# Lower weight halves of every second gate and up chunk, made by a ScalarE negation and an adding DMA

## The chip, the core and the metric

The kernel runs as one program on one core of a Trainium2 chip. The metric is the device time of one execution in microseconds (us). Before the change the median of 3 runs is 1681.12 us.

## What is computed

One layer of a decoder trunk on 256 tokens of width 2048, all in float32. Cut to what the change touches, it is

```python
h = h + _mixer(_rmsnorm(h, norm_mix[l]), ...)          # linear attention and convolution, merged
h = h + _swiglu(_rmsnorm(h, norm_ffn[l]), w_gate[l], w_up[l], w_down[l])

def _swiglu(h, w_gate, w_up, w_down):
    return (jax.nn.silu(h @ w_gate) * (h @ w_up)) @ w_down
```

The hidden width of the second part (the FFN) is 5632. `w_gate` and `w_up` are 2048 x 5632 each, 92 MB together.

## The kernel before

**Products in two parts.** TensorE takes its operands in a rounded float32 format (float32r in the code). To keep float32 accuracy every weight w is split into `hi` (w rounded to float32r) and `lo = w - hi`, every activation likewise, and three products are summed: hi.hi, hi.lo and lo.hi. In the form used by the gate and up weights (form "M"), a weight tile of 128 x 128 is held stationary; `hi` is multiplied with both halves of the activations at once (512 columns, L223), `lo` with the upper half alone (256 columns, L224).

**The weight stream.** The weights lie packed in HBM in groups of 2048 columns on 128 partitions, 1024 KB each. SyncE's queue (SP) loads one group by one DMA into a tile `raw` (L165); there are three such tiles (`RAW = 3`). A group holds two chunks of 1024 columns, and a chunk is the unit of all that follows. For each chunk ScalarE (ACT) makes `hi` by a casting copy (L175), VectorE (DVE) makes `lo` by a subtraction `raw - hi` (L177), and TensorE (PE) then runs 16 products on it, 2 rows of weight tiles by 4 tiles of output, each with its pair L223 and L224. `hi` and `lo` have five tiles each (`LOOK + 1`), so chunk i takes the tile of chunk i - 5 and can be split as soon as PE has finished that one, four chunks ahead of its use.

**The FFN.** Eleven blocks of 512 gate columns alternate with eleven blocks of up columns. A block runs over 2048 rows, that is 8 chunks or 4 groups, so gate and up together are 176 chunks in 88 groups. Behind the last chunk of a block stand four evacuations: ACT copies half of a bank (`ms`, L252), DVE adds the other half (`mt`, L256), multiplies by the norm, and ACT applies silu (`gt`) for gate, or ACT and DVE split the product into `hs` for up. The down projection that follows takes its weights from the same stream.

**What sets the order.** `run_blocks` writes, for each chunk of products, first the load and split of the chunk four ahead (`load_next`), then the products. A tile framework places the instructions on the engines and adds semaphore waits; each engine works its own list in order. GpSimd (POOL) does next to nothing: constants and four masks.

Of the kernel before, what the change touches and what calls it, by code (L numbers as in the profile page):

```python
# [8 lines left out]
F32 = mybir.dt.float32  # L9
F32R = mybir.dt.float32r  # L10
AF = mybir.ActivationFunctionType
ALU = mybir.AluOpType

P = 128
T = 256
D = 2048
KT = D // P
# [4 lines left out]
NB = 512  # L22
Q0, K0, V0, R0, A0, U0, G0, GA0, GB0 = 0, 1024, 2048, 4096, 6144, 6160, 8208, 10256, 12304
P_MIX, P_CB, P_LG, P_LB, P_PB, P_GN, P_NF, P_BA = [i * 16 for i in range(8)]
LOOK = 4     # chunks of weights split ahead of the products
RAW = 3      # groups of weights in flight
NA = 60      # slots of 2 KB for activations
NS = 8       # single-tile chunks at the start
WARM = 10    # products that bring the tensor engine to its clock
# background work let in per chunk, in the unit of the steps' costs  # L30
BUD, BG, BO = 1.22, 0.95, 1.05


# [1 line left out]
def trunk(ctx: ExitStack, tc, xT, par, convw, ws, wal2, nfin, out):  # L35
# [21 lines left out]

    v, sc, pe = nc.vector, nc.scalar, nc.tensor

# [1 line left out]
    pr = cpool.tile([P, 8 * 16], F32, tag="pr", name="pr")  # L61
    nc.scalar.dma_start(pr, par)
    ones = cpool.tile([P, P], F32, tag="ones", name="ones")
# [20 lines left out]
        return pr[:, off + i:off + i + 1]  # L84

    def split(dst, src):
        """dst [P, 512] F32R = (hi | lo) of src [P, 256]"""
        sc.copy(dst[:, 0:T], src)
        v.tensor_tensor(dst[:, T:2 * T], src, dst[:, 0:T].bitcast(F32), op=ALU.subtract)  # L89

# [1 line left out]
    tick = [0]  # L92
    order = {}
    done = set()

    class Work:
        """steps run in order; a step with a delay waits that many chunks after the one before"""

        def __init__(self):
            self.steps, self.last = deque(), 0  # L100
# [31 lines left out]
            q = gla_w_ if gla_w_.ready() else conv_w_  # L132
            credit[0] -= q.step()

# [1 line left out]
    # Products of float32: both operands split exactly into hi + lo float32r parts, summed as  # L136
    # hi.hi + hi.lo + lo.hi. Form "M": weights stationary, one bank holds W_hi.x_hi beside
    # W_hi.x_lo + W_lo.x_hi; form "S": the three in one region; form "A": x stationary.
    blocks = []

    def add_block(width, nk, form, xs, evac, before=None, budget=BUD):
        blocks.append(dict(width=width, nk=nk, form=form, xs=xs, evac=evac,
                           before=before, budget=budget))

    loads = []
    staged = {}
    nload = [0]
    raws = {}

    def load_next():  # L150
        i = nload[0]
        if i >= len(loads):
            return
        nload[0] += 1
        g, e, n, k, kp, width = loads[i]
        first = i < len(blocks[0]["chunks"])
        if 0 < i and first:
            x_load(k, kp)
        if first or e == 0:
            # a whole group of two chunks at once, but for the first block  # L160
            size = n if first else 2 * n
            raw = (atile([P, NB], s="raw") if kp == 1 else
                   wpool.tile([P, 4 * NB], F32, tag="raw", name=nm("raw"), bufs=RAW))
            with tc.issue_after(order["s"]) if "s" in order else nullcontext():
                d = nc.sync.dma_start(raw[:, 0:size], ws[g, :, e:e + size])  # L165
            raws["t"] = raw
            if i == 0:
                order["s"] = d.ins
        r0 = 0 if first else e
        r = raws["t"][:, r0:r0 + n]  # L170
        if i == 0:
            x_load(k, kp)
        hi, lo = (wpool.tile([P, kp, width], F32R, tag=t, name=nm(t)) for t in ("hi", "lo"))
        fl = lambda t: t.rearrange("p k n -> p (k n)")
        order["a"] = sc.copy(fl(hi), r).ins  # L175
        gs = [x_gain(j) for j in range(k, k + kp)] if first else []
        order["v"] = v.tensor_tensor(fl(lo), r, fl(hi).bitcast(F32), op=ALU.subtract).ins  # L177
        for x in gs:
            XU.append(atile([P, 2 * T], F32R, "xu"))
            with tc.issue_after(order["a"]), tc.issue_after(order["v"]):  # L180
                split(XU[-1], x)
        staged[i] = (hi, lo)

    def run_blocks():
        group = 0
        for b in blocks:
            b["first"] = len(loads)
            kp = 2 * NB // b["width"]
            b["chunks"] = [(k, kp) for k in range(0, b["nk"], kp)]
            if b is blocks[0]:  # L190
                b["chunks"] = [(k, 1) for k in range(NS)] + b["chunks"][NS // 2:]
            for k, kp in b["chunks"]:
                at = k * b["width"]
                loads.append((group + at // (4 * NB), at % (4 * NB), kp * b["width"], k, kp, b["width"]))
            group += b["nk"] * b["width"] // (4 * NB)
        for b in blocks:
# [49 lines left out]
                    pump(b["budget"])  # L246

    def merged_sum(a, bias=None):
        """the two halves of a bank, added"""
        t1 = ttile("ms")  # L250
        if bias is None:
            sc.copy(t1, a[:, 0:T])  # L252
        else:
            sc.activation(t1, a[:, 0:T], AF.Identity, bias=bias)
        t2 = ttile("mt")
        v.tensor_tensor(t2, a[:, T:2 * T], t1, op=ALU.add)  # L256
        return t2

    def rms_bcast(dst, acc_t, mat, eps):
        """dst = 1 / sqrt(column sums of acc_t through mat + eps), on every partition"""  # L260
        m = misc()
        pe.matmul(m[:, 0:T], lhsT=mat, rhs=acc_t, start=True, stop=True)  # L262
        s = ttile("rs")
        sc.activation(s, m[:, 0:T], AF.Sqrt, bias=eps)
        v.reciprocal(dst, s)

# [1 line left out]
    xp = []  # L268
    XU = []
    X = []  # L270
# [53 lines left out]
            X.append(s)  # L324
        return f

# [1 line left out]
    U = {}  # L328
    YC = {}
    US = {}  # L330
# [31 lines left out]
        return f  # L362

    def conv(p):
        """channel tiles 2p and 2p + 1, taps in turns"""
        def first(j):
            def f():
                if j == 0:
                    YC[p] = atile([P, 2, T], s="yc")
                i = 2 * p + j  # L370
                sc.activation(YC[p][:, j, :], u_tile(i), AF.Identity,
                              scale=cw[:, i, CW - 1:CW], bias=pcol(P_CB, i))
            return f

        def tap(d, j):
            def f():
                i = 2 * p + j
                y = YC[p][:, j, :]
                v.scalar_tensor_tensor(y[:, d:T], in0=u_tile(i)[:, 0:T - d],  # L379
                                       scalar=cw[:, i, CW - 1 - d:CW - d], in1=y[:, d:T],  # L380
                                       op0=ALU.mult, op1=ALU.add)
            return f
        conv_w_.add(0.0, first(0))
        conv_w_.add(0.0, first(1))
        for d in range(1, CW):
            for j in range(2):
                conv_w_.add(0.37, tap(d, j))
# [54 lines left out]
            conv_w_.add(1.3, scale(i))  # L442
        conv_w_.mark("conv")

# [1 line left out]
    QK = {}  # L446
    VT = {}
    SR = {}
# [37 lines left out]
        return t.rearrange("p j (c s) -> p (j c) s", s=64)  # L486

    def gla_att(h):
        """the masked, decayed scores of head h, keys on partitions"""
        st = ST[h]  # L490

        def z():
# [51 lines left out]
                sc.activation(dq[:, j], even[:, j], AF.Exp, scale=-1.0 / 16)  # L544
            st.update(dk=dk, dq=dq, qs=[], ks=[])

        # b: log decay from a chunk's start; the pair of chunks 0, 1 and the pair 2, 3 meet at
        # the border inside the pair, queries 2, 3 and keys 0, 1 at the border between the pairs
        def queries(j):
            def f():  # L550
                eb, q = (t[:, j, :].rearrange("p (c s) -> p c s", s=64) for t in (st["eb"], QK["q", h]))
                dq = st["dq"][:, j]
                a = atile([P, 6, 64], s="qs")
                # q0 -> border, q1, q2 -> border, q3, q2, q3 from chunk 2's start
                v.tensor_tensor(a[:, 0:4:2, :], q[:, 0::2, :], dq, op=ALU.mult)
                v.tensor_tensor(a[:, 1:4:2, :], q[:, 1::2, :], eb[:, 1::2, :], op=ALU.mult)
                v.tensor_tensor(a[:, 4, :], q[:, 2, :], eb[:, 2, :], op=ALU.mult)
# [4 lines left out]
        def prods(j):  # L562
            def f():
# [1 line left out]
                             for t in (st["eb"], st["dk"], QK["k", h]))  # L565
                en = st["en"][:, j]
                a = atile([P, 6, 64], s="ks")
                # kd0 ke1 kd0' kd1 kd2 ke3
                v.tensor_tensor(a[:, 0::4, :], k[:, 0::2, :], dk[:, 0::2, :], op=ALU.mult)
                v.tensor_tensor(a[:, 1::4, :], k[:, 1::2, :], en, op=ALU.mult)  # L570
                v.tensor_tensor(a[:, 3, :], k[:, 1, :], dk[:, 1, :], op=ALU.mult)
# [4 lines left out]
        def att():  # L576
            m = misc()
            qs, ks = st.pop("qs"), st.pop("ks")
            # keys 0:128 by queries 0:128, keys 128:256 by queries 128:256, keys 0:128 by queries 128:256
            for c, ko, qo in ((0, 0, 0), (1, 4, 2), (2, 2, 4)):  # L580
                for j in range(2):
                    pe.matmul(m[:, c * P:(c + 1) * P], lhsT=ks[j][:, ko:ko + 2, :],  # L582
# [21 lines left out]
        gla_w_.add(0.0, att, 2)  # L604

    def gla_out(h):
        """head h's output and its norm"""
        st = ST[h]

        def outp(pp):  # L610
# [49 lines left out]
            gla_w_.add(1.0, gate(e), 1)  # L660
        gla_w_.mark(("gla", h))

# [1 line left out]
    SGA, SGB = {}, {}  # L664
    MG = {}
    XR = {}
# [80 lines left out]
    def ffn_gate_evac(blk):  # L747
        def f(n, a):
            gla_w_.drain("rstd2")
            t = merged_sum(a)  # L750
            g = ttile("fg")
            v.tensor_tensor(g, t, rstd, op=ALU.mult)
            GT[n] = tpool.tile([P, T], F32, tag="gt", name=nm("gt"), bufs=5)
            sc.activation(GT[n], g, AF.Silu)
        return f
# [50 lines left out]
                nc.sync.dma_start(out[n * P:(n + 1) * P, m * NB:(m + 1) * NB], o)  # L806
        return f

# [1 line left out]
    xu = lambda: XU  # L810
    xx = lambda: X

# [39 lines left out]
    for blk in range(4):  # L852
        add_block(NB, KT, "M", lambda: MG, out_evac(blk), before=out_before(blk))
    for blk in range(11):
        add_block(NB, KT, "M", lambda: Y2, ffn_gate_evac(blk), budget=0.01)
        add_block(NB, KT, "M", lambda: Y2, ffn_up_evac(blk), budget=0.01)
    for nb in range(4):
        add_block(NB, HT, "A", lambda: HS, down_evac(nb),
                  before=down_before if nb == 0 else None, budget=0.0)
# [60 lines left out]
```

## Time and profile before

| | |
|---|---|
| median of 3 runs | 1681.12 us (1680.71 to 1681.37) |
| span of the profiled execution, first to last instruction | 1678.7 us |
| products of gate and up chunks | from 929.2 to 1430.2 us in the span |
| PE busy | 1666.4 us, 99% |
| DVE busy | 1219.4 us, 73% |
| ACT busy | 883.3 us, 53% |
| POOL busy | 4.5 us, 10 instructions |

The profiled execution's own time is given by its span; 2.4 us of the median lie around it. The page lists busy time by engine, the chain of work that ended last (followed back from the last instruction through what released each step), the costliest groups of instructions with the idle time before them, and the DMA queues. Idle time of an engine counts only where it lies on that chain.

### The profile page before, as it was taken

The numbers are of one execution on the slowest core, as the hardware profiler recorded it, in microseconds if no ns is written. First come the engines' busy times: TensorE is split into PE (matmuls) and PEld (weight loads), VectorE is DVE, ScalarE is ACT, GpSimd is POOL, SyncE is SP. The second block draws the span as 40 slices with busy tenths as digits, with TensorE's granted clock in tenths as the row PEclk, the third lists the DMA queues.
The fourth block names the chain that finished last, engine by engine and source line by source line (L and its number), as shares of the span: only waits on it lengthen the run. The fifth ranks groups of instructions, "written<-read, shape, count | busy, mean of one in ns | idle before, by whom it ended". The sixth has DMA issues, their size and how long they took to land.

```text
span 1678.7 us, 23321 instructions
## 1 busy us (share of the span) xinstructions
PE 1666.4 (99%) x9140; PEld 1437.8 (86%) x9140; DVE 1219.4 (73%) x1945; ACT 883.3 (53%) x1293; POOL 4.5 (0%) x10
## 2 busy tenths in 40 slices
PE   9999999999999999999999999999999999999997
PEld 7888888888888888888888888888888888888886
DVE  7898899888879899886777666666666666554453
ACT  6654444666766655584555654444444444444343
POOL 0000000000000000000000000000000000000000
PEclk9999999999999999999999999999999999999999
DMA  8555555554444445555555545555454555655552
GB/s 301 185 201 189 188 184 190 181 186 177 166 173 174 173 177 195 182 184 195 199 206 214 182 176 194 181 188 189 180 196 176 194 182 186 215 201 191 188 198 100
DMA packets 48413, 316.45 MB, mean 189 GB/s; under 512 B 5392, under 2 KB 6672, under 8 KB 11312
## 3 DMA queue, kind: packets, MB, share of 16 engines
q1 hardware_dynamic: 48160, 314.91, 52.2%
q8 instruction: 71, 1.16, 0.3%
q14 instruction: 38, 0.31, 0.1%
q10 hardware_dynamic: 144, 0.07, 0.0%
HBM read 312.86 MB, written 2.10 MB: 188 GB/s over the span
## 4 chain that ended last, share of the span: by engine, by line
PE 99%; DMA 0%; DVE 0%; ACT 0%; issue 0%; ACTq 0%; SPq 0%; DVEq 0%
PE acc L223 52%; PE acc L224 26%; PE acc L216 7%; PE acc L217 6%; PE acc L218 6%; PE m L582 0%; PE m L497 0%; PE m L619 0%; PE m L620 0%; DMA x<-in_xT_dram 0%; PE m L618 0%; PE m L740 0%; PE m L262 0%; PE acc L228 0%; PE acc L227 0%; PE acc L229 0%
## 5 line engine op out<-in xcount | busy, mean ns | idle before, releaser
L177 DVE TENSOR_TENSOR lo<-raw,hi 128x1024 fp32r<-128x1024 f32 (+1 forms) x590 | 717.1, 1216 | 412.2 <-ACT hi L175 406.1
L175 ACT CAST hi<-raw 128x1024 fp32r<-128x1024 f32 (+1 forms) x590 | 616.4, 1046 | 730.3 <-PE acc L223 523.2
L223 PE MATMUL acc<-y2s,hi 128*128 128x512 f32 x1408 | 498.4, 399 | 0.0
L223 PE MATMUL acc<-xs,hi 128*128 128x512 f32 x1280 | 450.5, 397 | 0.0
L224 PE MATMUL acc<-y2s,lo 128*128 128x256 f32 x1408 | 395.3, 281 | 0.0
L224 PE MATMUL acc<-xs,lo 128*128 128x256 f32 x1280 | 357.0, 279 | 0.0
L223 PEld LDWEIGHTS acc<-y2s,hi 128*128 128x128 f32 x1408 | 264.6, 188 | 65.4
L223 PEld LDWEIGHTS acc<-xs,hi 128*128 128x128 f32 x1280 | 240.3, 188 | 57.5 <-ACT hi L175 0.3
L224 PEld LDWEIGHTS acc<-y2s,lo 128*128 128x128 f32 x1408 | 265.9, 189 | 0.0
L224 PEld LDWEIGHTS acc<-xs,lo 128*128 128x128 f32 x1280 | 241.1, 188 | 0.1
L379 DVE SCALAR_TENSOR_TENSOR yc<-u,cw,yc 128x255 f32<-128x255 f32 (+14 forms) x480 | 199.6, 463 | 0.1
L216 PE MATMUL acc<-hi,hs 128*128 128x512 f32 x352 | 137.0, 389 | 0.0
L218 PE MATMUL acc<-hi,hs 128*128 128x512 f32 x352 | 136.9, 389 | 0.0
L217 PE MATMUL acc<-lo,hs 128*128 128x512 f32 x352 | 136.9, 389 | 0.0
L223 PE MATMUL acc<-xu,hi 128*128 128x512 f32 x256 | 90.3, 398 | 2.4 <-DVE xu L89 2.4
L223 PE MATMUL acc<-ogs,hi 128*128 128x512 f32 x256 | 89.3, 394 | 0.0
L223 PE MATMUL acc<-mgs,hi 128*128 128x512 f32 x256 | 88.8, 394 | 0.0
L223 PE MATMUL acc<-us,hi 128*128 128x512 f32 x256 | 88.8, 394 | 0.0
L256 DVE TENSOR_TENSOR mt<-acc,ms 128x256 f32<-128x256 f32 x200 | 81.6, 417 | 7.7 <-ACT ms L252 7.7
L218 PEld LDWEIGHTS acc<-hi,hs 128*128 128x128 f32 x352 | 66.1, 188 | 13.9
L216 PEld LDWEIGHTS acc<-hi,hs 128*128 128x128 f32 x352 | 66.1, 188 | 13.7
L217 PEld LDWEIGHTS acc<-lo,hs 128*128 128x128 f32 x352 | 66.1, 188 | 13.6
(176 smaller groups left out, 1607.4 us busy)
## 6 DMA issues: line engine op xcount, KB each, us to landing
raw<-in_weights_dram SPq DMA_DIRECT2D x289, 1024.0 KB, 4.8
raw<-in_weights_dram SPq DMA_DIRECT2D x8, 256.0 KB, 4.5
raw<-in_weights_dram SPq DMA_DIRECT2D x4, 512.0 KB, 7.0
xr<-in_xT_dram SPq DMA_DIRECT2D x8, 256.0 KB, 5.2
out_dram<-fin SPq DMA_DIRECT2D x8, 256.0 KB, 3.1
x<-in_xT_dram SPq DMA_DIRECT2D x8, 128.0 KB, 4.7
x<-in_xT_dram SPq DMA_DIRECT2D x4, 256.0 KB, 7.0
nf<-in_norm_final_dram SPq DMA_DIRECT2D x4, 256.0 KB, 6.6
```

Source lines behind the costliest of these rows:

```text
L175: order["a"] = sc.copy(fl(hi), r).ins
L177: order["v"] = v.tensor_tensor(fl(lo), r, fl(hi).bitcast(F32), op=ALU.subtract).ins
L216: pe.matmul(a, lhsT=xh[:, t], rhs=hi[:, kk, :], start=st, stop=False)
L217: pe.matmul(a, lhsT=xh[:, t], rhs=lo[:, kk, :], start=False, stop=False)
L218: last = pe.matmul(a, lhsT=xl[:, t], rhs=hi[:, kk, :], start=False, stop=en)
L223: pe.matmul(a, lhsT=wh, rhs=x, start=st, stop=False)
L224: last = pe.matmul(a[:, T:2 * T], lhsT=wl, rhs=xh, start=False, stop=en)
L256: v.tensor_tensor(t2, a[:, T:2 * T], t1, op=ALU.add)
L379: v.scalar_tensor_tensor(y[:, d:T], in0=u_tile(i)[:, 0:T - d], scalar=cw[:, i, CW - 1 - d:CW - d], in1=y[:, d:T], op0=ALU.mult, op1=ALU.add)
```

## The change

In gate and up blocks (`dma=True`), for the second chunk of each group (`k // kp % 2 == 1`), the subtraction on DVE is gone. In its place ACT writes `lo = -hi` by an activation with scale -1, and POOL's queue then issues a DMA from SBUF to SBUF that adds `raw` to `lo`. The first chunk of each group is split as before. 88 chunks are changed. The adding DMAs are kept in order among themselves. The diff also drops comments, which shifts line numbers (L177 becomes L184); those hunks are left out here.

```diff
-    def add_block(width, nk, form, xs, evac, before=None, budget=BUD):
+    def add_block(width, nk, form, xs, evac, before=None, budget=BUD, dma=False):
         blocks.append(dict(width=width, nk=nk, form=form, xs=xs, evac=evac,
-                           before=before, budget=budget))
+                           before=before, budget=budget, dma=dma))
...
         order["a"] = sc.copy(fl(hi), r).ins
         gs = [x_gain(j) for j in range(k, k + kp)] if first else []
-        order["v"] = v.tensor_tensor(fl(lo), r, fl(hi).bitcast(F32), op=ALU.subtract).ins
+        if by_dma[i]:
+
+            order["a"] = sc.activation(fl(lo), fl(hi).bitcast(F32), AF.Copy, scale=-1.0).ins
+            with tc.issue_after(order["g"]) if "g" in order else nullcontext():
+                order["g"] = nc.gpsimd.dma_start(fl(lo).bitcast(F32), r, accum_op=ALU.add).ins
+        else:
+            order["v"] = v.tensor_tensor(fl(lo), r, fl(hi).bitcast(F32), op=ALU.subtract).ins
...
             for k, kp in b["chunks"]:
                 at = k * b["width"]
+                by_dma.append(b["dma"] and k // kp % 2 == 1)
...
-        add_block(NB, KT, "M", lambda: Y2, ffn_gate_evac(blk), budget=0.01)
-        add_block(NB, KT, "M", lambda: Y2, ffn_up_evac(blk), budget=0.01)
+        add_block(NB, KT, "M", lambda: Y2, ffn_gate_evac(blk), budget=0.01, dma=True)
+        add_block(NB, KT, "M", lambda: Y2, ffn_up_evac(blk), budget=0.01, dma=True)
```

**ACT's list behind the end of an up block.** `hi_1904` and `hi_1910` are the two chunks of one group, `ms` and `hs` belong to the block that ends. Names in brackets are the semaphores that an instruction waits for: those with DMAHW are of SP's loads, those with DMASW of POOL's DMAs. Before:

```order
L175 CAST hi_1904_10228<-raw_1903_10226 128x1024 [waits DMAHW3_49,DVE_49,PE_49]
L88 CAST hs_1887_10178<-hd_1886_10176 128x256 [waits DVE_49]
L252 COPY ms_1888_10185<-acc_1863_10021 128x256
L175 CAST hi_1910_10252<-raw_1903_10226 128x1024 [waits PE_49,Activation_49]
L252 COPY ms_1893_10200<-acc_1864_10026 128x256 [waits Activation_49]
L88 CAST hs_1892_10193<-hd_1891_10191 128x256 [waits DVE_49]
L175 CAST hi_1913_10274<-raw_1912_10272 128x1024 [waits DMAHW4_49,PE_49]
```

With the change:

```order
L176 CAST hi_1904_10246<-raw_1903_10244 128x1024 [waits DMAHW3_49,PE_49]
L260 COPY ms_1893_10218<-acc_1864_10040 128x256 [waits Activation_49]
L88 CAST hs_1892_10211<-hd_1891_10209 128x256 [waits DVE_49]
L176 CAST hi_1910_10270<-raw_1903_10244 128x1024 [waits PE_49]
L260 COPY ms_1898_10233<-acc_1865_10045 128x256 [waits Activation_49]
L88 CAST hs_1897_10226<-hd_1896_10224 128x256 [waits DVE_49]
L180 ACTIVATE lo_1911_10271<-hi_1910_10270 128x1024 [waits DMASW5_49,PE_49,Activation_49]
L176 CAST hi_1913_10293<-raw_1912_10291 128x1024 [waits DMAHW4_49,PE_49]
```

One negation stands behind each second cast, here with one `ms` and one `hs` between the two; elsewhere in a block it follows the cast directly.

**SP's list of loads, at the same place.** Before, a load waits for the loads and for DVE, which is the last reader of the `raw` tile that it fills:

```order
L165 DMA raw_1873_10098<-in_weights_dram 128x2048 [waits DMAHW6_49,DVE_49]
L165 DMA raw_1878_10140<-in_weights_dram 128x2048 [waits DMAHW7_49,DVE_49]
L165 DMA raw_1903_10226<-in_weights_dram 128x2048 [waits DMAHW0_49,DVE_49]
L165 DMA raw_1912_10272<-in_weights_dram 128x2048 [waits DMAHW1_49,DVE_49]
L165 DMA raw_1917_10314<-in_weights_dram 128x2048 [waits DMAHW2_49,DVE_49]
```

With the change:

```order
L166 DMA raw_1873_10114<-in_weights_dram 128x2048 [waits DMASW5_49,DMAHW6_49,DVE_49,Activation_49]
L166 DMA raw_1878_10157<-in_weights_dram 128x2048 [waits DMASW6_49,DMAHW7_49,DVE_49,Activation_49]
L166 DMA raw_1903_10244<-in_weights_dram 128x2048 [waits DMASW7_49,DMAHW0_49,DVE_49,Activation_49]
L166 DMA raw_1912_10291<-in_weights_dram 128x2048 [waits DMASW0_49,DMAHW1_49,DVE_49,Activation_49]
L166 DMA raw_1917_10334<-in_weights_dram 128x2048 [waits DMASW1_49,DMAHW2_49,DVE_49,Activation_49]
```

Each load now waits for an adding DMA too: the one that reads the old contents of its `raw` tile, three groups back.

## Rows read from the trace of the kernel before

**Rows 1.** The page: busy us (share of the span) xinstructions; the chain's first line.

```profile
PE 1666.4 (99%) x9140; PEld 1437.8 (86%) x9140; DVE 1219.4 (73%) x1945; ACT 883.3 (53%) x1293; POOL 4.5 (0%) x10
...
PE 99%; DMA 0%; DVE 0%; ACT 0%; issue 0%; ACTq 0%; SPq 0%; DVEq 0%
```

**Rows 2.** Stretches of the span: window, then columns as its first line names them.

```profile
core 0: us, PE busy (x) PEld busy (x) DVE busy (x) ACT busy (x) POOL busy (x), PEclk, DMA share, GB/s
...
640.00:670.00 30.00, 30.00 (x175) 26.25 (x174) 28.34 (x53) 15.66 (x24) 0.00 (x0) 1.00 0.52 181
...
760.00:790.00 30.00, 30.00 (x175) 26.23 (x174) 19.16 (x27) 14.37 (x19) 0.00 (x0) 1.00 0.54 194
...
935.00:1430.00 495.00, 495.00 (x2818) 429.94 (x2817) 309.24 (x435) 241.29 (x358) 0.00 (x0) 1.00 0.52 185
```

**Rows 3.** Groups of instructions, 935 to 1430 us: busy us, mean ns | idle before, releasers.

```profile
L177 DVE TENSOR_TENSOR lo<-raw,hi 128x1024 fp32r<-128x1024 f32 x174 | 213.2, 1225 | 181.1 <-ACT hi L175 179.0
L175 ACT CAST hi<-raw 128x1024 fp32r<-128x1024 f32 x174 | 182.8, 1050 | 248.0 <-PE acc L223 230.2 <-issue 14.1 <-PE acc L224 2.1
...
L252 ACT COPY ms<-acc 128x256 f32<-128x256 f32 x86 | 31.3, 364 | 2.3 <-PE acc L224 2.3
...
L88 ACT CAST hs<-hd 128x256 fp32r<-128x256 f32 x40 | 16.2, 406 | 1.2 <-PE acc L224 1.2
...
L716 ACT ACTIVATE hq<-h 128x512 f32<-128x512 f32 x1 | 0.6, 629 | 0.0
```

**Rows 4.** ACT's timeline in an FFN block: start us, us, instruction, idle before.

```profile
1198.68 1.05 ACT L175 CAST hi<-raw 128x1024 fp32r<-128x1024 f32 x1 [1.76 <-PE acc L223]
1201.45 1.05 ACT L175 CAST hi<-raw 128x1024 fp32r<-128x1024 f32 x1 [1.73 <-PE acc L223]
...
1215.59 1.05 ACT L175 CAST hi<-raw 128x1024 fp32r<-128x1024 f32 x1 [1.44 <-PE acc L223]
```

**Rows 5.** DVE's timeline at the same place, and SP's waits from 935 to 1430 us.

```profile
1202.54 1.22 DVE L177 TENSOR_TENSOR lo<-raw,hi 128x1024 fp32r<-128x1024 f32 x1 [1.55 <-ACT hi L175]
...
SPq L165 <- DVE lo L177: 285.0, 54, 6.1
```

**Rows 6.** DMA, 935 to 1430 us: queue share of 16 engines; loads to landing.

```profile
q1 hardware_dynamic: 12100, 88.09, 50.9%
...
raw<-in_weights_dram SPq DMA_DIRECT2D x85, 1024.0 KB, 4.8
...
DMA to landing us min/median/max: 4.6/4.8/5.2
```

**Rows 7.** DMA in the first 40 us: slices of 1 us, queue share, landing times.

```profile
GB/s 0 27 144 285 351 327 293 272 262 327 373 346 350 217 203 301 406 424 408 358 184 311 246 180 360 369 303 311 394 376 438 409 240 156 332 410 295 238 418 393
...
q1 hardware_dynamic: 4393, 11.94, 87.2%
...
raw<-in_weights_dram SPq DMA_DIRECT2D x6, 1024.0 KB, 5.8
...
DMA to landing us min/median/max: 3.6/4.9/7.9
```

**Rows 8.** Short transfers, SP's issue, and POOL's longest instruction.

```profile
out_dram<-fin SPq DMA_DIRECT2D x8, 256.0 KB, 3.1
...
L165 SPq DMA_DIRECT2D raw<-in_weights_dram x87: 327/328/328, 940.5 to 1429.9; - x87
...
L587 POOL TENSOR_SCALAR_AFFINE_SELECT at<-at 128x256 f32<-128x256 f32 x4 | 3.8, 943 | 479.5 <-ACT at L585 479.5
```

More of the change, by code (lines that the diff above doesn't have):

```diff
@@ L139, in trunk @@
     blocks = []
-    def add_block(width, nk, form, xs, evac, before=None, budget=BUD):
+    def add_block(width, nk, form, xs, evac, before=None, budget=BUD, dma=False):
         blocks.append(dict(width=width, nk=nk, form=form, xs=xs, evac=evac,
-                           before=before, budget=budget))
+                           before=before, budget=budget, dma=dma))
     loads = []
+    by_dma = []
     staged = {}
```

## The prediction

> **What bounds the kernel now.** I read the busy times and the chain of waits first [rows 1]: the chain is 99% PE, so only what makes PE wait, or stop waiting, can move the time. Then the windows [rows 2]: over gate and up PE is busy in all 495.00 us and its granted clock is 1.00, the upper of its two levels, so there is no wait to remove and no clock to win. Nor does DVE's work slow PE's products down: the same 175 matmul records stand in 30 us whether DVE is busy 28.34 us or 19.16 us. That leaves slack as the question, and it is read from the timeline. Casts of `hi` follow each other at 2.82 us (from 1198.68 to 1215.59 in six steps, [rows 4]), each released by PE's last product on the tile of chunk i - 5. So a chunk takes 2.82 us, a group 5.64 us, and a cast starts four chunks, 11.3 us, ahead of the first product on its chunk. The subtraction that follows ends at 1203.76 [rows 5], 2.3 us after its cast began at 1201.45: 9.0 us to spare.
>
> **What is removed.** 88 subtractions of 1.225 us [rows 3], 107.8 us of DVE. None of it is on the chain, so it gives nothing.
>
> **What ACT gets.** 88 negations of 128x1024. The nearest rows are the cast of the same size, 1.05 us, and an activation of half the size, 0.629 us, which doubled is 1.26 us [rows 3]. I take 1.05 us, by size; 1.26 is the upper end. That is 92 us more in a stretch where ACT is busy 241.29 of 495 us [rows 2]. The cover is the 1.7 us that ACT waits for PE before each cast [rows 4]; without it each negation would cost 1.05 us. Behind a block's end one `ms` and one `hs` (0.364 and 0.406 us, [rows 3]) stand between cast and negation, so the negation ends 2.1 us after the cast's start, or 2.9 us there.
>
> **What the adding DMA costs.** No row shows one; POOL issues no DMA before. It has three parts.
> Issue: between SP's 0.33 us and POOL's longest instruction, 0.94 us [rows 8]. I take 1 us, since this is POOL's work.
> Bytes: an addition must read both operands, 512 KB of `raw` and 512 KB of `lo`, so its DMA reads as much as a load of 1024 KB, and it writes half as much. A load lands in 4.8 us and keeps the engines busy for 50.9% of 5.64 us, 2.87 us [rows 6]. The lower end is to count the 512 KB once, 1.44 us of engines; the other end is three passes, read, read and write, 4.3 us. I take two, 2.87 us, so 4.8 us to landing when alone.
> Company: in the FFN loads run one at a time, 4.6 to 5.2 us each [rows 6]. In the first 40 us, where transfers overlap, the same 1024 KB land in 5.8 us by the median, and the longest landing is 7.9 us [rows 7], 1.0 to 3.1 us more. Load and addition will overlap most of the time: 2.87 + 2.87 = 5.74 us of engine time stand against 5.64 us per group. (The engines can do somewhat better, 438 GB/s in the best slice of [rows 7] against 185 GB/s here, by which a load needs 2.4 us.) I take 2.0 us, the middle, for each.
> So the addition lands A = 1 + 4.8 + 2.0 = 7.8 us after its issue, and a load takes L = 4.8 + 2.0 = 6.8 us.
>
> **Which wait ends last.** There are two deadlines.
> The first is PE's: `lo` of a second chunk has 11.3 - 2.1 = 9.2 us from the negation's end, 8.4 us behind a block's end. A of 7.8 us meets both. Past it, a second chunk i starts late, but its tiles come free when PE ends chunk i - 5, a first chunk that directly follows second chunk i - 6. So a lateness is handed on over six chunks, that is three groups, and each us of it costs 88 / 3 = 29 us in all.
> The second is the `raw` tile's. Today SP's load waits for DVE's subtraction [rows 5]; with the change it waits for the addition to land, and every later load is queued behind it on SP. The round of a tile is load L, first cast 1.05, second cast 1.05, negation 1.05, some 0.2 us between engines, and A: 3.35 + L + A. Three tiles allow it 3 x 5.64 = 16.9 us, so L + A may be 13.55 us. I have 6.8 + 7.8 = 14.6 us: 1.05 us over, a third of it per group, times 88 groups, is **31 us**. The `hi` casts then wait for loads, their four chunks of lead are used up, and PE stalls at that rate.
> The ends: with the least company, L + A = 5.8 + 6.8 = 12.6, no stall, 0; with the most, 7.9 + 8.9 = 16.8, 3.25 x 29.3 = 95 us.
> The matmul's wait for `lo` changes its releaser from DVE to a DMA; the number of waits on PE stays, which I cost at nothing, hidden while `lo` is there first. The first chunks' subtractions keep their place.
>
> **Forecast.** On the profiled execution's 1678.7 us span the sum is 1678.7 + 31 = 1710; the median of the runs lies 2.4 us above its span, so 1712 us. Chance 0.42.
>
> **Rivals.**
> No change: the addition fits. For it: L + A needs only 1 us less than I assume, and at the best slice's rate both transfers need 4.8 of 5.64 us. If its bytes count once (1.44 us), A is about 5 us and everything is hidden. Time 1681, within 0.2% (about what a measurement of this kernel can tell from no change). The Trainium skill, DMA: Bandwidth & Descriptors, section Anatomy of one DMA, gives 2.0 us and the bytes at 436 GB/s for a DMA from this queue, an estimate of 3.2 us for 512 KB, by which the sum would be zero. Chance 0.37.
> Much slower: the adding path is a bottleneck of its own. It decides once an addition takes over 2.8 us of the engines, what a group leaves beside the load. At three passes, 4.3 + 2.87 = 7.17 us per group in place of 5.64: 1.53 x 88 = 135 us, 1816 us. For it: nothing shows that engines add at the rate they copy, and the rows of a chunk are half as long as a load's. Against: 438 GB/s were moved in the best slice. The Trainium skill, Collectives: The Full Stack, section The bandwidth ceiling, says that an addition costs a DMA two source reads on one ring and no more, so half the rate of a copy; by that the engines' price would be the 2.87 us taken above and this case would not occur, which no run here shows yet. Chance 0.17.
> Faster: PE's products gain from 108 us less of DVE, or from its ports. The equal 175 records at 28.34 and 19.16 us of DVE [rows 2] speak against it; were DVE the bound, at most 108 us would go, 1573 us. Chance 0.04.
> That the change doesn't do what it says is left out: 88 subtractions are gone from DVE's list, and 88 activations and 88 POOL DMAs are there.
>
> **How the numbers follow.** The likeliest case gives 1712 us. The range holds the case of no change, down to 1678, and the forecast to its upper end, 1681 + 95 = 1776, taken as 1780; outside lie the heavy case and the gain. That holds some 0.8. Slower by over 0.2% is 0.42 + 0.17 = 0.59, within 0.2% 0.37, faster 0.04.
>
> **What would show it.** In the profile after, the DVE group of subtractions is down by 88, an ACT group of 88 negations stands at 1.0 to 1.3 us, and the DMA share of gate and up rises from 0.52 towards 1. If the forecast holds, loads land in over 6 us, ACT's casts name the load of `raw` as what they waited for, and PE has idle time released by casts or subtractions of first chunks as well. If PE waits for the addition alone, and casts still wait for PE, the first deadline failed and not the second. Right for no change: PE stays busy in every slice, and a load's landing plus the addition's stays below 13.5 us. I am wrong in kind if the addition lands far later than 9 us though the engines are not full, since then issue on POOL, not bytes, is the price.

## The result: slower by 2.8%

The changed kernel takes 1725.04 us by the median of 5 runs (1721.11 to 1743.92), the kernel before 1681.12. The ratio is 1.0277, 95% interval 1.0254 to 1.0301: 43.9 us more. The profiled execution is the longest of the five, 1743.92 us with a span of 1742.2 us, so the trace shows some 19 us more than the median does. Its mean granted clock, 0.989, is also the lowest; the other four have 0.993 to 0.997.

The page of the changed kernel: busy us (share of the span) xinstructions, then the first two lines of the chain that ended last. They answer to [rows 1].

```profile
PE 1684.9 (97%) x9140; PEld 1448.9 (83%) x9140; DVE 1116.4 (64%) x1857; ACT 965.8 (55%) x1381; POOL 79.3 (5%) x98
...
PE 71%; DMA 20%; issue 5%; ACT 2%; DVE 1%; SPq 0%; POOL 0%; POOLq 0%; ACTq 0%
PE acc L231 34%; PE acc L232 17%; DMA lo<-raw 11%; DMA raw<-in_weights_dram 9%; PE acc L224 6%; PE acc L226 6%; PE acc L225 6%; ACT hi L176 1%; DVE lo L184 0%; PE m L590 0%; PE m L505 0%; ACT lo L180 0%; PE m L627 0%; PE m L628 0%; PE m L626 0%
```

DVE lost 103 us and the time grew. The chain was 99% PE; now 20% of it is DMA, half additions (`lo<-raw`) and half loads (`raw<-in_weights_dram`). The window from the first to the last product of gate and up, columns as in [rows 2], in the kernel before and then in the changed one:

```profile
929.30:1430.50 501.20, 501.20 (x2853) 435.40 (x2852) 314.90 (x446) 245.17 (x366) 0.00 (x0) 1.00 0.51 185
...
929.30:1493.90 564.60, 520.93 (x2853) 447.00 (x2852) 213.09 (x357) 325.11 (x450) 73.74 (x87) 0.97 0.92 247
```

Gate and up take 63.4 us longer (564.60 - 501.20), which is all but 0.1 us of what the span grew by: the program before and behind them kept its times. PE idles 43.7 us there (564.60 - 520.93) where it idled none, and is busy 19.7 us longer for the same 2853 records. The granted clock is 0.97, and the DMA share rose from 0.51 to 0.92. Who waited for whom from 930 to 1490 us (us in total, times, longest; PEld is PE's weight load, which waits ahead of the product), and below it SP's own waits, against [rows 5]:

```profile
ACT hi L176 <- DMA raw<-in_weights_dram: 187.9, 70, 7.8
...
PEld acc L232 <- DMA lo<-raw: 51.7, 32, 3.6
PE acc L232 <- DMA lo<-raw: 41.3, 28, 3.3
ACT hi L176 <- PE acc L231: 20.1, 16, 5.2
...
SPq L166 <- DMA lo<-raw: 515.7, 87, 10.0
```

Read from below: SP's loads wait for additions, 87 times. ACT's casts, which had waited 230 us for PE in [rows 3], now wait 187.9 us for loads. And PE's `lo` products wait for additions. The DMA queues over the same stretch, against [rows 6] (q0 is POOL's):

```profile
q1 hardware_dynamic: 12672, 92.34, 48.1%
q0 software_dynamic: 12528, 45.62, 43.8%
...
raw<-in_weights_dram SPq DMA_DIRECT2D x88, 1024.0 KB, 7.0
lo<-raw POOLq DMA_DIRECT2D x87, 512.0 KB, 8.0
...
DMA to landing us min/median/max: 4.7/8.0/11.4
```

A load lands in L = 7.0 us (4.8 before), an addition in A = 8.0 us, counted from the start of POOL's instruction; the last line is of additions alone.

### The profile page after: what moved, and what is told of

It reads as the page before. It is cut to its first block, busy times and chain, and to the rows that moved or that the text cites. A ratio compares the mean times of both kernels' runs of the same rounds, so it can differ in the third digit from the quotient of the medians.

```text
span 1742.2 us, 23701 instructions
## 1 busy us (share of the span) xinstructions
PE 1684.9 (97%) x9140; PEld 1448.9 (83%) x9140; DVE 1116.4 (64%) x1857; ACT 965.8 (55%) x1381; POOL 79.3 (5%) x98
## 4 chain that ended last, share of the span: by engine, by line
PE 71%; DMA 20%; issue 5%; ACT 2%; DVE 1%; SPq 0%; POOL 0%; POOLq 0%; ACTq 0%
PE acc L231 34%; PE acc L232 17%; DMA lo<-raw 11%; DMA raw<-in_weights_dram 9%; PE acc L224 6%; PE acc L226 6%; PE acc L225 6%; ACT hi L176 1%; DVE lo L184 0%; PE m L590 0%; PE m L505 0%; ACT lo L180 0%; PE m L627 0%; PE m L628 0%; PE m L626 0%
## 5 line engine op out<-in xcount | busy, mean ns | idle before, releaser
L184 DVE TENSOR_TENSOR lo<-raw,hi 128x1024 fp32r<-128x1024 f32 (+1 forms) x502 | 609.7, 1215 | 565.8 <-ACT hi L176 554.3
L231 PE MATMUL acc<-y2s,hi 128*128 128x512 f32 x1408 | 509.5, 404 | 0.0
L232 PE MATMUL acc<-y2s,lo 128*128 128x256 f32 x1408 | 405.3, 288 | 41.6 <-DMA lo<-raw 41.3
L231 PEld LDWEIGHTS acc<-y2s,hi 128*128 128x128 f32 x1408 | 271.5, 193 | 63.0
L232 PEld LDWEIGHTS acc<-y2s,lo 128*128 128x128 f32 x1408 | 273.6, 194 | 51.8 <-DMA lo<-raw 51.7
L182 POOL DMA_DIRECT2D lo<-raw x88 | 74.8, 850 | 918.7 <-ACT lo L180 713.5
L180 ACT ACTIVATE lo<-hi 128x1024 fp32r<-128x1024 f32 x88 | 93.1, 1058 | 1.4
```

Of the source, the lines that this page charges most:

```text
L180: order["a"] = sc.activation(fl(lo), fl(hi).bitcast(F32), AF.Copy, scale=-1.0).ins
L182: order["g"] = nc.gpsimd.dma_start(fl(lo).bitcast(F32), r, accum_op=ALU.add).ins
L231: pe.matmul(a, lhsT=wh, rhs=x, start=st, stop=False)
L232: last = pe.matmul(a[:, T:2 * T], lhsT=wl, rhs=xh, start=False, stop=en)
```

## The experiments

Three theories. The first is the forecast's: the `raw` tile's round (load L, two casts, negation, addition A) is longer than three tiles allow. The second is that PE's deadline fails: the addition lands too late for the product however early the load came. The third: the DMA engines are simply full. Every excess below is the median less that of the kernel before, run beside it.

**1. The addition in the first chunk of a group.**

```diff
-                by_dma.append(b["dma"] and k // kp % 2 == 1)
+                by_dma.append(b["dma"] and k // kp % 2 == 0)
```

> Edit: the first chunk of each group is the one that the adding DMA completes, not the second. The addition is then issued one cast (1.05 us) earlier in the round of its raw tile, so the round is 2.3 + L + A in place of 3.35 + L + A. Theory 1 (the raw tile's round is the deadline that fails; the changed kernel shows L = 7.0, A = 8.0 us): L + A may now be 14.6 us, 0.4 us over or less, so the excess over the kernel before falls from 44 us to 5 to 20 us. Theory 2 (PE's own deadline fails: the addition lands later than 9.2 us after its issue): that lead is the same for a first chunk, so the excess stays at 35 to 50 us. Theory 3 (the DMA engines are simply full): the bytes are the same, 35 to 50 us as well.

Measured: 1699.19 us, ratio 1.0109 (1.0079 to 1.0139), excess 18.3 us. One cast less in the round takes away more than half of the loss with the same bytes, which speaks for the first theory. The landing times from 930 to 1430 us and the waits from 930 to 1460 us:

```profile
raw<-in_weights_dram SPq DMA_DIRECT2D x85, 1024.0 KB, 6.7
lo<-raw POOLq DMA_DIRECT2D x84, 512.0 KB, 7.2
...
ACT hi L176 <- DMA raw<-in_weights_dram: 40.7, 17, 5.2
PEld acc L232 <- DMA lo<-raw: 22.1, 26, 2.7
```

Casts wait for loads 17 times in place of 70, and PE still waits for additions. L + A is 13.9 us here, under the 14.6 that this round allows, so by the forecast's formula the tile costs nothing any more. What the remaining 18.3 us are is taken up in experiment 9.

**2. Four raw tiles.**

```diff
-RAW = 3
+RAW = 4
-NA = 60
+NA = 57
```

> Edit: RAW 3 to 4, with NA 60 to 57 to make room (6 KB fewer for activations). Theory 1: four tiles allow a round of 22.6 us, L + A up to 19.2 us against the 15.0 us measured, so casts no longer wait for loads and the excess falls from 44 us to 0 to 10 us; what is left is additions that land past 9.2 us. Theory 2: the lead of the split is the same, so 35 to 50 us stays. Theory 3: the engines had 92% busy in gate and up; if that is full, more tiles do not help and 30 us or more stays, with the DMA share still above 0.9.

Measured: 1691.50 us, ratio 1.0083 (1.0052 to 1.0114), excess 10.6 us. The window 930 to 1430 us and the waits from 930 to 1460 us of this kernel:

```profile
930.00:1430.00 500.00, 493.12 (x2791) 425.66 (x2790) 207.77 (x350) 325.46 (x445) 73.13 (x87) 1.00 1.00 271
...
ACT hi L176 <- PE acc L231: 173.2, 146, 1.9
...
PEld acc L232 <- DMA lo<-raw: 15.1, 26, 1.3
```

Its DMA queues from 930 to 1430 us, the last line for additions alone:

```profile
q1 hardware_dynamic: 12343, 89.98, 53.1%
q0 software_dynamic: 12384, 45.09, 46.3%
...
raw<-in_weights_dram SPq DMA_DIRECT2D x86, 1024.0 KB, 6.6
...
DMA to landing us min/median/max: 4.8/7.9/10.7
```

No cast waits for a load any more; they wait for PE again, as before the change. Three quarters of the loss went with the tile's round, though the DMA share is now 1.00: full engines alone, the third theory, do not cost the 44 us. What is left is PE waiting for additions, 15.1 us in 26 waits. They still land in 7.9 us by the median and 10.7 at most, so some pass PE's deadline (9.2 us from the negation's end, 8.4 behind a block's end). Full engines may have a part in this rest: load and addition take 3.09 and 2.66 us of the engines here (53.1% of 500 us by 86, 46.3% by 87), 5.75 us per group, and the kernel before took 501.2 / 88 = 5.70 us for a group. No run separates the two.

**3. One more chunk of lead for PE.**

```diff
-LOOK = 4
+LOOK = 5
-NA = 60
+NA = 57
```

> Edit: LOOK 4 to 5 (six hi and lo tiles, the split may start five chunks ahead), with NA 60 to 57. Theory 2: PE's deadline grows by one chunk, 2.82 us, to 12 us, past the longest landing of 11.4 us, so the excess falls from 44 us to under 5 us. Theory 1: the raw tiles' round contains no hi or lo tile, so the excess stays, 35 to 50 us. Theory 3: stays, 35 to 50 us.

Measured: 1738.80 us, ratio 1.0340 (1.0318 to 1.0362), excess 57.9 us. The waits from 930 to 1495 us:

```profile
ACT hi L176 <- DMA raw<-in_weights_dram: 180.9, 66, 7.8
...
PEld acc L232 <- DMA lo<-raw: 50.9, 28, 4.2
```

A longer lead for the split does not help where the load is late; PE still waits 50.9 us for additions and ACT 180.9 us for loads. The second theory falls as the cause of the 44 us. The excess is 8 us over the top of what the first theory expected, and by the medians more than the change itself. The change was not run again beside it, and its own five runs reach 1743.92 us, above this median. In the kernel before, the smaller room costs nothing (experiment 8); whether the difference is real stays open.

**4. The addition on a tile that nothing reads.** The addition left in place, and no product that waits for it:

```diff
-NA = 60
+NA = 57
...
-            order["a"] = sc.activation(fl(lo), fl(hi).bitcast(F32), AF.Copy, scale=-1.0).ins
+            side = wpool.tile([P, kp * width], F32, tag="side", name=nm("side"), bufs=2)
+            sc.activation(side, fl(hi).bitcast(F32), AF.Copy, scale=-1.0)
+            order["v"] = v.tensor_tensor(fl(lo), r, fl(hi).bitcast(F32), op=ALU.subtract).ins
...
-                order["g"] = nc.gpsimd.dma_start(fl(lo).bitcast(F32), r, accum_op=ALU.add).ins
+                order["g"] = nc.gpsimd.dma_start(side, r, accum_op=ALU.add).ins
```

> Edit: lo of every chunk is made by DVE's subtraction as before the change; the negation and the adding DMA still run for every second chunk of gate and up, but on a tile that nothing reads (two of them, NA 60 to 57). PE then never waits for an addition; only the raw tile does. Theory 1: the loads still wait for the additions, so at least half of the excess stays, 20 to 45 us, and the casts wait for loads. Theory 2: no excess, 0 to 4 us. Theory 3: 20 to 45 us, since the engines carry the same bytes.

Measured: 1739.13 us, ratio 1.0346 (1.0310 to 1.0383), excess 58.2 us. This is the plainest of them: PE never waits for an addition, the subtractions are all back on DVE, and the loss is there in full. SP's waits from 930 to 1430 us, then who waited from 930 to 1440 us:

```profile
SPq L166 <- DMA side<-raw: 471.4, 78, 10.8
...
ACT hi L176 <- DMA raw<-in_weights_dram: 172.7, 62, 6.2
...
PEld acc L234 <- DVE lo L186: 23.8, 28, 1.1
PEld acc L233 <- ACT hi L176: 19.4, 14, 3.1
```

It goes from the addition to the load, from the load to the cast and the subtraction, and from these to PE. The transfers are kept, so this run alone does not tell the first theory from the third; experiment 2 does. The 58 us are above the expected 20 to 45. Four waits of POOL for an earlier side addition (24.5 us) are new here and may be part of it; the rest stays open, as in experiment 3.

**5. ACT's negation alone.**

```diff
-            with tc.issue_after(order["g"]) if "g" in order else nullcontext():
-                order["g"] = nc.gpsimd.dma_start(fl(lo).bitcast(F32), r, accum_op=ALU.add).ins
+            order["v"] = v.tensor_tensor(fl(lo), r, fl(lo).bitcast(F32), op=ALU.add).ins
```

> Edit: the negation on ACT stays in every second chunk of gate and up, but DVE adds raw to it; no DMA adds anything. It is ACT's part of the change alone. Theory 1 (raw tile's round through the adding DMA): the round has only a negation more than before, 88 x 1.06 us lie in ACT's idle time, so 0 to 3 us over the kernel before. A rival that the longer list of ACT costs something itself: 10 us or more.

Measured: 1680.09 against 1679.96 us, ratio 0.9999 (0.9978 to 1.0020). The 88 negations cost nothing that these runs can tell; ACT is busy 329.04 us from 930 to 1430 us.

**6. A copy in place of the addition.**

```diff
-                order["g"] = nc.gpsimd.dma_start(fl(lo).bitcast(F32), r, accum_op=ALU.add).ins
+                order["g"] = nc.gpsimd.dma_start(fl(lo).bitcast(F32), r).ins
```

> Edit: POOL's DMA copies raw to lo in place of adding it, so lo holds the weights themselves and not their lower parts (the addition is left out, the waits stay). It tells what the second read costs. If an addition takes the engines about twice a copy (my step on bytes): the share of POOL's queue in gate and up falls from 43.8% to about 22 to 25%, the landing from 8.0 to 5 to 6.5 us, L + A below 13.5 us, and the excess from 44 us to 0 to 5 us. If the addition itself costs nothing beside the copy (bytes count once, the rest is the queue): the share stays over 38%, the landing near 8 us and the excess at 35 to 50 us.

Measured: 1680.59 us, ratio 1.0015 (0.9994 to 1.0036), excess 0.6 us. The queues from 930 to 1430 us, and below them a wait from 930 to 1440 us:

```profile
q1 hardware_dynamic: 12698, 92.49, 53.7%
q0 software_dynamic: 12528, 45.62, 23.7%
...
raw<-in_weights_dram SPq DMA_DIRECT2D x88, 1024.0 KB, 6.0
lo<-raw POOLq DMA_DIRECT2D x87, 512.0 KB, 5.4
...
ACT hi L176 <- DMA raw<-in_weights_dram: 77.6, 46, 5.7
```

What waits for what is as in the change, and so are the bytes written; only the addition, and with it the second read, is left out. One copy takes the engines 1.36 us (23.7% of 500 us, by 87). L + A is 11.4 us, below the 13.55 that three tiles allow, and the loss is gone. Casts wait for loads even so, 46 times, while PE waits 2.3 us for copies in all: the four chunks of lead cover such waits here.

**7. Additions for every fourth chunk.**

```diff
-                by_dma.append(b["dma"] and k // kp % 2 == 1)
+                by_dma.append(b["dma"] and k // kp % 4 == 1)
```

(In the code these are the second chunks of every second group. The expectation calls them first chunks and halves 18 us; half of what second chunks cost is 22 us.)

> Edit: the adding DMA for every fourth chunk only (the first chunk of every second group), 44 additions in place of 88; the other 44 chunks are subtracted on DVE again. Theory 1: the raw tile that waits for an addition is one in two, the engines carry a quarter less, so loads land in about 5.5 us, additions in about 6 to 7 us, and the excess is 0 to 3 us. If each addition cost a fixed delay whatever the traffic, half of the 18 us that additions in first chunks cost, 9 us, would stay.

Measured: 1679.61 us, ratio 0.9992 (0.9969 to 1.0016); neither 9 nor 22 us stay. The queues from 930 to 1430 us, the last line for additions alone:

```profile
q0 software_dynamic: 6192, 22.55, 23.9%
...
raw<-in_weights_dram SPq DMA_DIRECT2D x88, 1024.0 KB, 5.4
lo<-raw POOLq DMA_DIRECT2D x43, 512.0 KB, 4.8
...
DMA to landing us min/median/max: 4.5/4.8/5.3
```

This is the price of an addition with little company: 4.8 us from issue to landing, and 2.78 us of the engines (23.9% of 500 us, by 43). That is 2.04 times a copy.

**8. The kernel before with less room.** The control for `NA = 57`, which experiments 2 to 4 and 9 need.

> Edit: the kernel before with NA 57 in place of 60, the room that three of the experiments took. A control: what it costs is to be taken off their excess. All theories: 0 to 6 us.

Measured: 1680.75 us, ratio 1.0002 (0.9975 to 1.0029), an interval of some 5 us to either side. Nothing is to be taken off.

**9. Four raw tiles and the addition in the first chunk**, the edits of 1 and 2 together.

> Edit: four raw tiles (NA 57) and the addition in the first chunk of each group, both mends of the raw tile's round at once: the round may be 22.6 us and is 2.3 + L + A, some 17 us. It tells what the 11 us are that four tiles alone left. If they are PE's deadline (additions that land later than 9.2 us, because the engines are full), the lead is the same and 5 to 15 us stay, with PE waiting for additions and no cast waiting for a load. If they are a rest of the tile's round, they go: 0 to 3 us.

Measured: 1702.12 us, ratio 1.0130 (1.0094 to 1.0165), excess 21.0 us, above the 5 to 15 expected. The waits from 930 to 1460 us:

```profile
ACT hi L176 <- PE acc L231: 182.3, 151, 4.7
...
PEld acc L232 <- DMA lo<-raw: 20.5, 17, 2.6
```

No cast waits for a load, so this is no rest of the tile's round. PE waits for additions, 20.5 us in 17 waits, the longest 2.6 us, against 26 waits of at most 1.3 us with the addition in second chunks. So late additions do cost PE something once the tile's round is met. With three tiles the same additions cost 18.3 us (experiment 1), no more than with four, so what was left there is most likely all of this kind. Why first chunks miss PE's deadline by more was not settled, and no run gave PE one more chunk of lead beside four tiles.

## Why the prediction was right, and where it was not

**Direction and mechanism: right.** PE bound, no gain from 108 us of DVE, the loss through the `raw` tile's round: experiments 2 and 4 show this from both sides, one by adding a tile, the other by keeping of the addition only its transfer and the tile's wait. The fourth tile takes away 33 us (43.9 - 10.6), near the 31 that the forecast gave to this wait.

**Bytes: right.** I took two reads, 2.87 us of engines for one addition; it measures 2.78, and a copy 1.36. The one-read end of the range, under which I had put "no change", is experiment 6, and there nothing is lost. The heavy case needs over 2.8 us of engines per addition to set in and was missed by little: the share was 0.92 in the change, and 1.00 once a fourth tile let the transfers run. The Trainium skill's rule in Collectives: The Full Stack (section The bandwidth ceiling), two source reads and so half of a copy's rate, agrees: 2.04. The Trainium skill's 2.0 us plus bytes at 436 GB/s, from DMA: Bandwidth & Descriptors (section Anatomy of one DMA), gave an estimate of 3.2 us for 512 KB; the trace has 4.8 for an addition.

**Landing times: the sum nearly right by luck, its terms not.** Alone I took 1 us for issue and 4.8 to landing, 5.8 in all; the landing with little company is 4.8, POOL's issue included (experiment 7). For company I took 2.0 us each; it measures 3.2 for the addition (8.0 - 4.8) and 2.2 for the load (7.0 - 4.8). The errors cancel: together L + A is 15.0 against my 14.6, and the formula makes 29.3 x (15.0 - 13.55) = 42 us of it in place of 31. That this lies near 43.9 us is no proof of it. L and A are read from the profiled execution, which lost 63.5 us, and two terms were left out, the two that follow.

**PE's deadline: wrong.** I called it met because the median A of 7.8 us lies under 8.4. The landing reaches 11.4 us, and it is the late ones that PE meets: 10.6 us are left with four tiles, with the part of full engines in them open.

**The clock: left out.** I wrote that there was no clock to win and did not ask whether there was one to lose. The next section shows it; the span's granted clock fell from 0.999 to 0.989 in the profiled execution.

**What PE waits for: half right.** I expected casts and subtractions of first chunks among PE's releasers as well. All of the 51.7 us are additions. As I read it, first chunks have 9.0 us to spare [rows 5] and absorb a late load, and the lateness shows at the second chunk, whose chain of cast, negation and addition starts late too; no run tests this apart.

**ACT: right.** 1.058 us for a negation (1.05 taken), hidden, 0.1 us in all (experiment 5).

## What to carry to other kernels

Moving work from an instruction that is not on the chain to a DMA trades 1.2 us of an engine for 8 us of a buffer's time here: ask first who else holds the source tile, and write down the round of that tile (load, every reader, the DMA) against tiles times period, with landing times under the load that the change itself makes. Count both operands of an adding DMA as reads: it took the engines 2.04 times a copy. Where a round fails, one more buffer tells it from a deadline of the consumer in one run; fewer such DMAs do not, for they shorten the landing as well (8.0 to 4.8 us in experiment 7).

## What the runs showed of the hardware

**TensorE's clock fell behind the longer waits.** PE's timeline around two waits of the changed kernel, and windows behind the first (start us, us; window, PE, PEld, DVE, ACT and POOL busy, PEclk, DMA share, GB/s):

```profile
1227.82 0.40 PE L231 MATMUL acc<-y2s,hi 128*128 128x512 f32 x1
...
1228.17 0.40 PE L231 MATMUL acc<-y2s,hi 128*128 128x512 f32 x1
1231.73 0.39 PE L232 MATMUL acc<-y2s,lo 128*128 128x256 f32 x1 [3.16 <-DMA lo<-raw]
...
1233.05 0.63 PE L231 MATMUL acc<-y2s,hi 128*128 128x512 f32 x1
...
1233.69 0.63 PE L231 MATMUL acc<-y2s,hi 128*128 128x512 f32 x1
...
1482.77 0.58 PE L232 MATMUL acc<-y2s,lo 128*128 128x256 f32 x1 [3.30 <-DMA lo<-raw]
1483.15 0.63 PE L231 MATMUL acc<-y2s,hi 128*128 128x512 f32 x1
...
1233.00:1236.40 3.40, 3.40 (x13) 2.92 (x12) 0.00 (x0) 0.00 (x0) 0.49 (x1) 0.51 0.97 288
1236.40:1240.00 3.60, 3.60 (x23) 3.12 (x22) 0.01 (x1) 1.09 (x2) 0.00 (x0) 1.00 0.99 253
```

PE stood idle for 3.16 us, ran on at the upper level (2.4 GHz), then from about 1233 to 1236 us at the lower (1.2 GHz) though it was busy throughout, and then rose again. Behind the wait of 3.30 us it was at the lower level at once. A pair of products takes 0.64 us at the lower level (1233.05 to 1233.69) against 0.35 at the upper (1227.82 to 1228.17), so each us there loses 0.45. A mean of 0.989 in place of 0.999 over 1742 us is 35 us at the lower level, which is half the upper, and so 16 us lost. That is most of the 19.7 us that PE is busy longer over gate and up; some 4 us of these are not placed. With PE's 43.7 us of idle time they make up 63.4 of the 63.5 us between the two profiled spans. Where the longest idle time of PE was 1.0 us (experiment 2) the clock of gate and up did not fall; with 2.4 us (experiment 1) it fell once, for some 3 us; with 3.8 us (experiment 3) the span's clock was 0.991. That the waits bring the clock down is read from these rows; no run kept PE busy through a wait.

**POOL spends more on an adding DMA than on a copying one:** 850 ns each (74.8 us for 88) against 529 ns for the copies of experiment 6.
